# Seven-product blocks for the output projection and the first MLP product, and a norm ahead of its transposes

## The chip, the core and the metric

The kernel runs on one core of a Trainium2 chip. The time is device microseconds of one execution; smaller is better. The core has a matrix engine (TensorE, "PE" in the profile, its weight loads "PEld"), VectorE ("DVE"), ScalarE ("ACT"), GpSimd ("POOL"), and SyncE ("SP"), which issues plain DMAs. GpSimd's queue issues the DMAs that add into their destination. Every engine executes its own instructions in order; semaphores tie the engines together.

## The reference

One layer of a decoder over 512 rows of 1024 columns, all float32:

```python
def rms_norm(x, g):
    y = x * rsqrt(mean(x * x, axis=-1, keepdims=True) + EPS)
    return y * g

def reference(x, ...):
    h = rms_norm(x, norm_mix_g)
    p = h @ w_in                          # 1024 x 8208
    ...                                   # y_a: mLSTM heads, y_b: stick-breaking attention heads, sigmoid gates
    y = gates[..., :D] * y_a + gates[..., D:] * y_b
    x = x + y @ w_out                     # output projection, 1024 x 1024
    h2 = rms_norm(x, norm_mlp_g)
    x = x + square(relu(h2 @ w_up)) @ w_down      # 1024 x 4096, 4096 x 1024
    return x
```

The change touches only the last three lines: the output projection, the second norm, and the two products of the MLP with the way they are interleaved.

## The kernel before

**Numbers.** Every large product is made of three passes: an operand is split into a high part (rounded to the matrix engine's float32r) and a low part (the rest), and `mm3` adds high x high, high x low and low x high. A split costs one copy on ScalarE and one subtraction on VectorE (`stage` for weights, L102 and L103; `parts` in `down`, L695 and L696; `split`, L164 and L165). Weight tiles are 128 x 1024; the pool `wp` has two raw buffers, four of high parts (`whi`) and four of low parts (`wlo`), so weights of two products can stand ready.

**Order.** The framework plans an order for each engine from the program order, a priority and its own estimate of times. A block under `high_priority(offset=AHEAD)` is drawn ahead: weight loads and their splits are. Pools hand out buffers by tag; a new tile of a tag waits until the old tile's last reader is done. `late.close()` ends attention's pool `at`, and the pool `mp` takes over its SBUF.

**Attention's tail.** `ORDER` lists the steps; it ends with heads `s4` to `s7` and the gate chunk `gb1`. A head is a chain: products into `zb`, sigmoids, masks on POOL, scans, a product of vectors, transposes into `zt`, splits into `ah` and `al`, products into `po`, a copy to `yb` (L505). `b_gate_` then multiplies by the gate (L532), adds to `ya` (L533) and splits into `y`. `ya` is the sum of both branches, one 128 x 512 tile for each of eight heads, that is, eight blocks of 128 columns of y, transposed.

**Output projection.** `wo_chunk(half)` makes 512 columns: four row tiles, eight heads each, three passes, 96 matmuls of 128 x 512. The result is added to `acc_t` (L594), four 128 x 1024 tiles that were loaded with x by POOL (L586). A square with an accumulator (L596) gives the row sums of the norm.

**Second norm.** `h2_rows(k)` transposes a block of 128 columns of `acc_t` (L604) and splits it, scaled by the norm's weight (L605, L606). The row factor is applied later: it is spread over a 128 x 512 tile `rw` by products with a diagonal (L632 to L635), and multiplied in when the up product is emptied (L650).

**MLP.** `up(i)` makes 512 of the 4096 hidden columns, transposed, with 96 matmuls of 128 x 512, then relu, square and, for the next step, sums of its quarters. `down(g, u)` multiplies 1024 hidden columns by their 1024 x 1024 of `w_down` and adds to `acc_t`. It uses seven products in place of eight: both matrices are cut into quadrants (A11 to A22, B11 to B22), and each product takes a quadrant or a sum of quadrants. Sums of A are made on VectorE; sums of B by DMAs that add into the raw weight tile (`accum_op`, L719): buffer X holds B11 and then takes in more quadrants, Y holds B22, Z holds B21. `PRODUCTS` lists, for each product, the operand of A, the buffer of B, what is added to it first, and the PSUM tiles (x, z, y), in which products accumulate: 1 and 2 in x, 5 and 3 in z, 6, 7 and 4 in y. Between two products of one PSUM pair the sum so far is read out. `down(g)` yields between products 6 and 7, and there `up(2g + 2)` is put in; `up(2g + 3)` follows.

## Time and profile before

| | |
|---|---|
| runs | 840.05, 840.44, 842.07 us; median 840.44 |
| profiled execution | 838.94 us, span 837.2 us |
| PE busy, matmuls | 823.9 us (98%), 3798 |
| DVE busy | 564.0 us (67%) |
| ACT busy | 408.9 us (49%) |
| POOL busy | 125.9 us (15%) |
| DMA | 98.36 MB, mean 117 GB/s |
| HBM | read 95.52 MB, written 2.17 MB |

The span is the time from the program's first instruction to its last; the execution's time has some 1.7 us around it. Matmuls are pipelined: the duration shown for one includes time in which the next runs already, so the spacing of starts is what a stream costs. A line of the time by stretches gives the stretch, its length, and for each engine the busy time with the number of instructions, then the granted clock of TensorE, the DMA engines' share and their rate. A line in order of time gives start, duration, engine, line of the kernel, operation, out<-in with shapes, and in brackets the idle time ahead of it with what ended it. A line of the groups gives the count, the busy time, the mean duration of one in ns, and the idle time ahead of them. A line of DMA issues gives the tile, the queue, the count, the size of each and the median time from issue to landing.

### The profile page before, as it was taken

The numbers are of one execution on the slowest core, as the hardware profiler recorded it, in microseconds if no ns is written. First come the engines' busy times: TensorE is split into PE (matmuls) and PEld (weight loads), VectorE is DVE, ScalarE is ACT, GpSimd is POOL, SyncE is SP. The second block draws the span as 40 slices with busy tenths as digits, with TensorE's granted clock in tenths as the row PEclk, the third lists the DMA queues.
The fourth block names the chain that finished last, engine by engine and source line by source line (L and its number), as shares of the span: only waits on it lengthen the run. The fifth ranks groups of instructions, "written<-read, shape, count | busy, mean of one in ns | idle before, by whom it ended". The sixth has DMA issues, their size and how long they took to land.

```text
span 837.2 us, 10133 instructions
## 1 busy us (share of the span) xinstructions
PE 823.9 (98%) x3798; PEld 679.3 (81%) x3798; DVE 564.0 (67%) x776; ACT 408.9 (49%) x619; POOL 125.9 (15%) x181
## 2 busy tenths in 40 slices
PE   8999999999999999999999999999999999999997
PEld 5878877788888788888888888888888888888885
DVE  6479997796457786566456446774848475857684
ACT  6338467754436554363345336452545254434441
POOL 3012245142111110010111100020013001300130
PEclk9999999999999999999999999999999999999999
DMA  5163333342113242232122562287438654853374
GB/s 204 53 186 137 111 98 114 105 160 90 55 58 101 60 117 89 88 101 79 50 99 75 184 247 97 80 174 173 141 87 167 160 151 88 170 144 101 51 136 116
DMA packets 56067, 98.36 MB, mean 117 GB/s; under 512 B 4745, under 2 KB 17081, under 8 KB 56018
## 3 DMA queue, kind: packets, MB, share of 16 engines
q1 hardware_dynamic: 45298, 73.51, 27.5%
q0 software_dynamic: 10720, 24.20, 14.7%
q8 instruction: 30, 0.49, 0.2%
q14 instruction: 19, 0.16, 0.1%
HBM read 95.52 MB, written 2.17 MB: 117 GB/s over the span
## 4 chain that ended last, share of the span: by engine, by line
PE 47%; issue 37%; DMA 6%; DVE 5%; POOL 4%; ACT 1%; POOLq 0%; SPq 0%; DVEq 0%; ACTq 0%
DMA raw_X<-in_w_down_dram 5%; PE pp_qkb L107 3%; PE pp_qkb L109 3%; PE pp_qkb L108 3%; POOL raw_X L719 2%; PE pp_ga L107 2%; PE pp_vb L107 2%; PE pp_ga L109 2%; PE pp_ga L108 2%; PE pp_vb L108 2%; PE pp_gb L107 2%; PE pp_oa L107 2%; PE pp_gb L108 2%; PE pp_vb L109 2%; PE pp_oa L108 2%
## 5 line engine op out<-in xcount | busy, mean ns | idle before, releaser
L108 PE MATMUL pp_up<-hT,whi_up 128*128 128x512 f32 x256 | 99.7, 389 | 0.0
L107 PE MATMUL pp_up<-hT,whi_up 128*128 128x512 f32 x256 | 99.4, 390 | 0.0
L109 PE MATMUL pp_up<-hT,wlo_up 128*128 128x512 f32 x256 | 96.2, 389 | 0.0
L719 POOL DMA_DIRECT2D raw_X<-in_w_down_dram x24 | 29.0, 1209 | 287.6 <-DVE wlo_p L696 285.7
L103 DVE TENSOR_TENSOR wlo_up<-raw_up,whi_up 128x1024 fp32r<-128x1024 f32 x32 | 39.2, 1224 | 35.9 <-ACT whi_up L102 35.6
L102 ACT CAST whi_up<-raw_up 128x1024 fp32r<-128x1024 f32 x32 | 33.8, 1055 | 57.6 <-PE y L109 35.6
L109 PEld LDWEIGHTS pp_up<-hT,wlo_up 128*128 128x128 f32 x256 | 48.1, 188 | 10.0
L108 PEld LDWEIGHTS pp_up<-hT,whi_up 128*128 128x128 f32 x256 | 48.1, 188 | 9.9
L107 PEld LDWEIGHTS pp_up<-hT,whi_up 128*128 128x128 f32 x256 | 48.1, 188 | 9.9
L695 ACT CAST whi_p<-raw_X 128x1024 fp32r<-128x1024 f32 x32 | 33.8, 1056 | 37.7 <-PE pp_up L108 24.9
L107 PE MATMUL pp_qkb<-whi_qkb,hT 128*128 128x512 f32 x128 | 50.0, 393 | 0.2 <-DVE va L165 0.2
L482 POOL TENSOR_SCALAR_AFFINE_SELECT b<-b 128x128 f32<-128x128 f32 x32 | 21.2, 679 | 192.7 <-ACT b L479 114.9
L108 PE MATMUL pp_qkb<-wlo_qkb,hT 128*128 128x512 f32 x128 | 50.1, 391 | 0.0
L650 DVE SCALAR_TENSOR_TENSOR ur<-pp_up,rw 128x512 f32<-128x512 f32 x32 | 21.5, 690 | 42.0 <-PE pp_up L109 42.0
L109 PE MATMUL pp_qkb<-whi_qkb,hT 128*128 128x512 f32 x128 | 49.4, 391 | 0.0
L696 DVE TENSOR_TENSOR wlo_p<-raw_X,whi_p 128x1024 fp32r<-128x1024 f32 x32 | 39.1, 1223 | 6.1 <-ACT whi_p L695 5.9
L651 ACT ACTIVATE ur<-ur 128x512 f32<-128x512 f32 x32 | 19.5, 629 | 41.9 <-DVE ur L650 41.6
L487 DVE TENSOR_TENSOR_SCAN r<-r,msk 128x512 f32<-128x512 f32 (+3 forms) x32 | 25.6, 835 | 10.1 <-ACT r L478 10.1
L107 PEld LDWEIGHTS pp_qkb<-whi_qkb,hT 128*128 128x128 f32 x128 | 24.0, 188 | 5.6 <-DVE va L165 0.5
L109 PEld LDWEIGHTS pp_qkb<-whi_qkb,hT 128*128 128x128 f32 x128 | 24.0, 188 | 5.5
L108 PEld LDWEIGHTS pp_qkb<-wlo_qkb,hT 128*128 128x128 f32 x128 | 24.0, 188 | 5.3
L695 ACT CAST whi_p<-raw_Y 128x1024 fp32r<-128x1024 f32 x16 | 16.9, 1053 | 21.5 <-PE x L109 13.8
(290 smaller groups left out, 2310.0 us busy)
## 6 DMA issues: line engine op xcount, KB each, us to landing
raw_up<-in_w_up_dram SPq DMA_DIRECT2D x32, 512.0 KB, 4.0
raw_X<-in_w_down_dram POOLq DMA_DIRECT2D x24, 512.0 KB, 6.3
raw_qkb<-in_w_in_dram SPq DMA_DIRECT2D x32, 256.0 KB, 3.8
rb<-rows POOLq DMA_DIRECT2D x8, 640.0 KB, 4.9
raw_va<-in_w_in_dram SPq DMA_DIRECT2D x8, 512.0 KB, 6.5
raw_qka<-in_w_in_dram SPq DMA_DIRECT2D x16, 256.0 KB, 4.3
raw_vb<-in_w_in_dram SPq DMA_DIRECT2D x8, 512.0 KB, 4.0
raw_oa<-in_w_in_dram SPq DMA_DIRECT2D x8, 512.0 KB, 3.9
```

The source lines that it names most:

```text
L102: act.copy(hi, raw)
L103: dve.tensor_sub(lo, raw, hi.bitcast(F32))
L107: pe.matmul(o, ah, bh, start=start, stop=False, **kw)
L108: pe.matmul(o, ah, bl, start=False, stop=False, **kw)
L109: pe.matmul(o, al, bh, start=False, stop=stop, **kw)
L482: pool.affine_select(out=b[:, d], in_=b[:, d], pattern=[[-1, P]], compare_op=ALU.is_gt, fill=0.0, base=0, channel_multiplier=1)
L487: dve.tensor_tensor_scan(kr, kr, msk[:, S - n:][:, ::-1], 1.0, ALU.mult, ALU.max)
L650: dve.scalar_tensor_tensor(u[:, w, :], acc[j + 2 * w], 0.0, rw, ALU.max, ALU.mult)
L651: act.activation(u[:, w, :], u[:, w, :], AF.Square)
L695: act.copy(hi, t)
L696: dve.tensor_sub(lo, t, hi.bitcast(F32))
L719: pool.dma_start(out=buf[b, j], in_=src(more, j), accum_op=ALU.add)
```

## The change

- A function `wino` does one block of seven products for any weights, in the order 1, 2, 5, 3, 6, 7, 4. The output projection is one such block (168 matmuls of 128 x 512), each of the four groups of 1024 hidden columns one for the up product and one for the down product. In the up block the weights are the stationary operand and 256 rows stream: 48 matmuls of 128 x 256 for a product.
- `ya` becomes two tiles `yq` of 128 x 4 x 512 (heads 0 to 3, and 4 to 7). A11 and A12 are the first 256 rows of each. `rows_ops` makes A22, S1, S4, S2 and S3 in place, with four sums and five splits of 128 x 1024.
- The row factor of the second norm is applied to `acc_t` (a new tile `xh`) ahead of the transposes, for 256 rows at a time: rows 0 and 1 after product 6 of the projection, rows 2 and 3 after product 4. `rw` and its products go.
- The transposed rows go to `hq`, the up product is emptied into `uq`; `yq`, `hq` and every `uq` share the tags `ya0` and `ya1`, with one buffer each.
- `up` and `down` follow one another without interleaving in the program order. The raw buffers in `mp` go from eight to six; the block's first-freed weights (X in the projection, Z elsewhere) use the two raw buffers of `wp`.
- GpSimd's space for DMA descriptors is set to 4096.

```diff
+TARGET = {2: ((0, 0), 1), 5: ((1, 1), 1), 3: ((0, 1), 1), 6: ((0, 1), -1), 7: ((1, 1), -1), 4: ((1, 0), 1)}
+ORDER_W = (1, 2, 5, 3, 6, 7, 4)
+DONE = {2: (0, 0), 6: (0, 1), 7: (1, 1), 4: (1, 0)}
...
+    yq = [big.tile([P, 4, S], F32, tag=f"ya{c}", name=f"yq{c}") for c in range(2)]
+    ya = [yq[h // 4][:, h % 4, :] for h in range(8)]
...
+        a = f"A1{i + 1}"
+        Y[a] = rows_split(r4_pair(f"y{a}"), y_quad(0, i))      # at the end of b_gate_
...
+    def rows_split(pair, val):
+        hi, lo = pair
+        act.copy(hi, val)
+        dve.tensor_sub(lo, val, hi.bitcast(F32))
+        return pair
...
+    def wino(name, src, A, rows, emit, small, psum, first_load=None):
+        buf, sums = {}, {}
+        with ExitStack() as es:
+            es.enter_context(tc.high_priority(offset=AHEAD))
+            if first_load is not None:
+                es.enter_context(tc.issue_after(first_load))
+            for b, n in (("X", "B11"), ("Z", "B21"), ("Y", "B22")):
+                for j in range(2):
+                    pool_, tag, bufs = (wp, "raw", 2) if b == small else (mp, "rawd", 6)
+                    buf[b, j] = pool_.tile([P, 2, S], F32, tag=tag, name=f"raw_{b}{name}{j}", bufs=bufs)
+                    last["load"] = nc.sync.dma_start(out=buf[b, j], in_=src(n, j)).ins
...
+        for n in ORDER_W:
+            a, b, more, to = PRODUCTS[n]
+            with tc.high_priority(offset=AHEAD):
+                if n > 3:
+                    for j in range(2):
+                        pool.dma_start(out=buf[b, j], in_=src(more, j), accum_op=ALU.add)
+                w = [parts(f"p{n}{name}{j}", buf[b, j]) for j in range(2)]
+            start = to not in sums
+            if start:
+                sums[to] = [psum(f"{to}{name}{t}") for t in range(2)]
+            hi_a, lo_a = A[a]
+            for t in range(2):
+                for p in range(4):
+                    (hi, lo), kk = w[p // 2], p % 2
+                    if rows:
+                        sl = slice(t * P, (t + 1) * P)
+                        mm3(sums[to][t], hi_a[:, p, sl], lo_a[:, p, sl], hi[:, kk, :], lo[:, kk, :], ...)
+                    else:
+                        for o in range(2):
+                            sl = slice((2 * t + o) * P, (2 * t + o + 1) * P)
+                            mm3(sums[to][t][:, o * HT:(o + 1) * HT], hi[:, kk, sl], lo[:, kk, sl], hi_a[:, p, :],
+                                lo_a[:, p, :], ...)
+            for t in range(2):
+                emit(n, t, sums[to][t])
+            yield n
+
+    def rows_ops(A, q, tile):
+        A["A22"] = rows_split(tile("A22"), q(1, 1))
+        dve.tensor_sub(q(1, 1), q(1, 0), q(1, 1))
+        A["S1"] = rows_split(tile("S1"), q(1, 1))
+        dve.tensor_sub(q(1, 0), q(0, 0), q(1, 0))
+        dve.tensor_sub(q(0, 0), q(1, 1), q(0, 0))
+        dve.tensor_add(q(0, 1), q(0, 1), q(0, 0))
+        A["S4"] = rows_split(tile("S4"), q(0, 1))
+        A["S2"] = rows_split(tile("S2"), q(0, 0))
+        A["S3"] = rows_split(tile("S3"), q(1, 0))
...
+    def wo_emit(n, t, p):
+        for q, sign in SIGN_1.items() if n == 1 else [TARGET[n]]:
+            add(quad(*q, t), p, sign)
...
+    def h2_rows(r):
+        xh = []
+        for t in (2 * r, 2 * r + 1):
+            n = mp.tile([P, D], F32, tag="xh", name=f"xh{t}", bufs=2)
+            ss = sm.tile([P, 1], F32, tag="r1", name=f"ss{t}")
+            act.activation(n, acc_t[t], AF.Square, accum_out=ss)
+            act.activation(ss, ss, AF.Sqrt, scale=1.0 / D, bias=eps)
+            dve.reciprocal(ss, ss)
+            dve.tensor_scalar_mul(n, acc_t[t], ss)
+            xh.append(n)
+        ...                    # 16 transposes into four banks, eight scaled copies of 128 x 256 into hq
+
+    rows_ops(Y, y_quad, lambda name: r4_pair(f"y{name}"))
+    for n in wino("wo", weights(w_out, 0, 0), Y, True, wo_emit, "X", pp):
+        if n == 6:
+            h2_rows(0)
+            for c in range(2):
+                a = f"A1{c + 1}"
+                H2[a] = rows_split(h2_tile(a), h_quad(0, c))
+    wo_load = last["load"]
+    h2_rows(1)
+    rows_ops(H2, h_quad, h2_tile)
...
+    def up(g):
+        uq = [big.tile([P, 4, S], F32, tag=f"ya{c}", name=f"uq{g}{c}") for c in range(2)]
+        ...
+        def emit(n, t, p):
+            ...
+            if n == 1:
+                act.copy(h(1, 0), p)
+            elif n == 2:
+                act.activation(h(0, 0), p, AF.Relu)
+            elif n == 5:
+                dve.tensor_sub(h(1, 1), p, h(1, 0))
+            ...                # 3, 6, 7, 4: one sum or difference on VectorE each
+            if t == 1 and n in DONE:
+                ...            # maximum with 0 on VectorE, square on ScalarE, split of A11 and A12
+        for _ in wino(f"up{g}", weights(w_up, 0, g * D), H2, False, emit, "Z", pp, wo_load if g == 0 else None):
+            pass
+        rows_ops(U, q, tile)
+        return U
...
     for g in range(4):
-        nu = []
-        for _ in down(g, u):
-            nu += up(2 * g + 2)
-        u = nu + up(2 * g + 3) if g < 3 else []
+        down(g, up(g))
...
-    nc = _bacc.Bacc("TRN2", target_bir_lowering=False, num_devices=1)
+    nc = _bacc.Bacc("TRN2", target_bir_lowering=False, num_devices=1, dynamic_dma_scratch_size=4096)
```

211 lines of the change are left out of this document (89 added, 122 removed), and 3 rows, old and new, of the table PRODUCTS.

## The prediction

> **What bounds the kernel now.** I read the page's engine table and slices first, then the time by stretches, then the order of instructions in time at the two places that the change rebuilds.
>
> ```profile
> PE 823.9 (98%) x3798; PEld 679.3 (81%) x3798; DVE 564.0 (67%) x776; ACT 408.9 (49%) x619; POOL 125.9 (15%) x181
> PE   8999999999999999999999999999999999999997
> PEclk9999999999999999999999999999999999999999
> ```
>
> TensorE is busy 823.9 of 837.2 us, in every slice but the first and last, at full clock. So each matmul taken away is worth its spacing, provided that nothing else then runs dry. A matmul's duration (389 ns for 512 columns) overlaps its neighbour's; what counts is the spacing of starts.
>
> ```profile
> core 0: us, PE busy (x) PEld busy (x) DVE busy (x) ACT busy (x) POOL busy (x), PEclk, DMA share, GB/s
> 580.00:620.00 40.00, 40.00 (x178) 33.14 (x177) 22.26 (x34) 15.64 (x23) 0.00 (x0) 1.00 0.41 127
> 792.50:833.60 41.10, 39.27 (x170) 31.23 (x168) 30.19 (x42) 14.90 (x18) 7.27 (x6) 1.00 0.65 134
> ...
> 239.44 0.28 PE L107 MATMUL po<-ah,vb 128*128 128x256 f32 x1
> 239.56 0.29 PE L108 MATMUL po<-al,vb 128*128 128x256 f32 x1
> 239.68 0.28 PE L109 MATMUL po<-ah,vb 128*128 128x256 f32 x1
> 239.80 0.39 PE L384 MATMUL za<-qh,kk 128*128 128x512 f32 x1
> ...
> 465.19 0.28 PE L107 MATMUL po<-ah,vb 128*128 128x256 f32 x1
> 465.30 0.28 PE L108 MATMUL po<-al,vb 128*128 128x256 f32 x1
> 465.42 0.28 PE L109 MATMUL po<-ah,vb 128*128 128x256 f32 x1
> 465.53 0.22 PE L107 MATMUL po<-ah,vb 128*128 128x128 f32 x1
> ```
>
> The first window holds only 512-column matmuls: 40.00/178 = 0.225 us each. Three 256-column ones take 0.36 us at 239.44 and 0.34 us at 465.19: 0.113 to 0.12, mean 0.117, a little over half. The second window is the last down block, the only seven-product block with no up chunk beside it.
>
> **The change part by part.** *TensorE work.* The output projection goes from 2 chunks x 4 x 8 x 3 = 192 matmuls to 7 products x 2 x 4 x 3 = 168, all of 512 columns: 24 x 0.225 = 5.4 us less. The up product goes from 8 x 96 = 768 of 512 columns (172.6 us) to 4 groups x 7 products x 48 = 1344 of 256 columns: 1344 x 0.117 = 157 us, 15.6 less (ends: at 0.12, 11.3 less; at 0.113, 20.7). So seven products of eight bring 9%, not 12.5%, since a half-width matmul costs more than half. The transposes stay 32; the products that made rw go:
>
> ```profile
> L634 PE MATMUL prw<-dg,ones 128*128 128x128 f32 x8 | 1.1, 274 | 0.0
> ```
>
> Together 5.4 + 15.6 + 1.1 = 22.1 us less. In a kernel that is 98% TensorE that would be 818. The rest asks what TensorE then waits for.
>
> [...]
>
> *Ahead of the output projection.* Now the tail of attention is covered by it: head 7 is a chain of transposes, copies and sums, and the projection's products over heads 0 to 6 fill TensorE meanwhile.
>
> ```profile
> 451.90:457.30 5.40, 5.36 (x23) 4.13 (x23) 0.00 (x0) 1.00 0.03 9
> 451.90:475.00 23.10, 20.68 (x89) 16.41 (x90) 0.52 (x1) 1.00 0.27 97
> ...
> 466.63 0.69 DVE L532 TENSOR_TENSOR g_gb<-g_gb,yb 128x512 f32<-128x512 f32 x1 [4.78 <-ACT yb L505]
> 467.36 0.69 DVE L533 TENSOR_TENSOR ya<-ya,g_gb 128x512 f32<-128x512 f32 x1
> ...
> 468.69 2.13 POOL L586 DMA_DIRECT2D acc<-in_x_dram  x4 [16.62 <-issue]
> ...
> 477.13 0.69 DVE L594 TENSOR_TENSOR acc<-acc,pp_wo 128x512 f32<-128x512 f32 x1 [1.37 <-DMA acc<-in_x_dram]
> 478.45 0.69 DVE L594 TENSOR_TENSOR acc<-acc,pp_wo 128x512 f32<-128x512 f32 x1 [0.63 <-DMA acc<-in_x_dram]
> ```
>
> The first two rows count the projection's matmuls alone: 20.68 us of them between 451.9 and 475. Afterwards only product 1 (A11, heads 0 to 3) is possible before head 7's y is added at 468.05, because A12 and all sums need heads 4 to 7: 24 x 0.225 = 5.4 us. The remaining 15.3 us of cover are gone. Work resumes near 475: from 468.05, two copies on ScalarE of A12 and A22 and, on VectorE, A12's and A22's low parts, one difference, then S1's copy and low part:
>
> ```profile
> L696 DVE TENSOR_TENSOR wlo_p<-raw_X,whi_p 128x1024 fp32r<-128x1024 f32 x32 | 39.1, 1223 | 6.1 <-ACT whi_p L695 5.9
> L695 ACT CAST whi_p<-raw_X 128x1024 fp32r<-128x1024 f32 x32 | 33.8, 1056 | 37.7 <-PE pp_up L108 24.9 <-PE z L109 4.8 <-PE x L109 4.8
> 636.11 1.23 DVE L696 TENSOR_TENSOR wlo_p<-raw_X,whi_p 128x1024 fp32r<-128x1024 f32 x1
> 637.25 0.69 DVE L165 TENSOR_TENSOR ta<-sa,ta 128x512 fp32r<-128x512 f32 x1
> 637.85 0.69 DVE L165 TENSOR_TENSOR tb<-sb,tb 128x512 fp32r<-128x512 f32 x1
> ```
>
> 1.06, three VectorE steps at their spacing of 1.14 (636.11 to 637.25), 1.06 and 1.22: 468.05 + 6.8 = 474.8, when product 5 can start. Its added weights need an adding load on POOL's queue, which holds little there: head 7's masks before 452 and the four acc loads, 2.13 us. Product 2 is no earlier. Its weights (Z) lie in pool mp, whose first load was issued at 468.69, right after attention's last read of the SBUF that mp takes over; and it adds into product 1's banks, which must first be emptied into acc, whose last rows landed about 477 and 478, with Z and Y, which wait on SP's queue for the same release, now loading beside them. So I take 15.3 us lost; ends 10 (head 7 sooner, ScalarE and VectorE having fewer copies of y beside it) and 22 (product 2 first, at 482).
>
> *The second norm.* Now each block of columns is transposed unscaled and the row factor is applied after the up product, so no matmul waits for the norm. Then it stands ahead of the transposes. Rows 0 and 1 are done under products 7 and 4 (10.8 us). Rows 2 and 3 start when product 4 ends:
>
> ```profile
> L594 DVE TENSOR_TENSOR acc<-acc,pp_wo 128x512 f32<-128x512 f32 x8 | 5.4, 686 | 9.5 <-PE pp_wo L109 7.5 <-DMA acc<-in_x_dram 2.0
> L216 ACT ACTIVATE jk<-x 128x1024 f32<-128x1024 f32 x4 | 4.2, 1060 | 2.7 <-DMA x<-in_x_dram 2.7
> L217 ACT ACTIVATE r<-r,eps 128x1 f32<-128x1 f32 x4 | 1.2, 295 | 0.2
> L218 DVE RECIPROCAL r<-r 128x1 f32<-128x1 f32 x4 | 0.6, 157 | 4.6 <-ACT r L217 4.6
> L334 DVE TENSOR_SCALAR cy<-xc,vec 128x512 f32<-128x512 f32 x8 | 4.1, 528 | 2.8 <-ACT xc L328 2.8
> L604 PE MATMUL p<-ident,acc 128*128 128x128 f32 x32 | 4.6, 272 | 0.0
> L654 ACT CAST ue<-ur 128x256 fp32r<-128x256 f32 x32 | 11.2, 397 | 0.0
> ```
>
> Matmul's end 0.4, add 0.7, square 1.06, its accumulator 0.2, root 0.3, reciprocal 0.16, scaling of 1024 columns about 1.0, first transposes 0.7, eight copies at 0.4: quadrants complete 7.6 us after product 4. Then nine VectorE operations of 1.14 (four differences and sums, five low parts; the price of 128x1024 above), one copy ahead and two weight splits between: 12.5 + 1.06, so the last sum is split at about +21. The up block can run products 1 and 5 meanwhile (2 x 48 x 0.117 = 11.2) and 16 transposes (about 1.6), but not product 2: product 1's banks are emptied into uq, which has the SBUF tag of hq with a single buffer, so that copy waits until the last operand is split from hq. Cover 12.8, wait 21.6 with the copy: 9 us lost. Ends: 0 (uq free as soon as S1 is there, at about +13) and 14.6 (product 5 not drawn ahead of product 2, another 5.6).
>
> *Seven-product up blocks.* The 256-column products come every 5.6 us and each needs two weight splits (2 x 1.06 on ScalarE, 2 x 1.14 on VectorE). An up and a down block together: 28 weight splits, seven operand splits and four sums, all at 1.14 = 44.5 us, plus 23 emptyings at the 0.6 from 637.25 to 637.85 and three maxima of 1024 at about 1.0 (twice the 0.53 of L334) = 16.8: 61.3 us of VectorE in 77 us, 80%. In the last down block, at 30.19/41.10 = 73%, TensorE lost 41.10 - 39.27 = 1.8 us. I take that for the four up blocks, 7 us; the down blocks have an up block's first product behind them as filler, as now. Ends: 0 and 12.6 (the other three down blocks too).
>
> *DMAs.* Up and projection weights gain 8 adding loads per block in place of plain ones:
>
> ```profile
> raw_X<-in_w_down_dram POOLq DMA_DIRECT2D x24, 512.0 KB, 6.3
> q1 hardware_dynamic: 45298, 73.51, 27.5%
> q0 software_dynamic: 10720, 24.20, 14.7%
> ```
>
> An adding load lands 6.3 us after issue; from the split of a product's weights to the same buffer's next is two products, 11 us, less the split's 2.4: hidden, with 2 us to spare. Shares: 40 more on q0 (21 MB, +13%), 10 fewer on q1 (5 MB, -2%): 42 to 53% over the span, no bound by itself. POOL issues 8 x 1.2 us per block; nothing else stands in that queue then. At nothing, covered by those 11 us; without, it is in the blocks' upper end. The smaller descriptor space for POOL's DMAs shows in no row; 0, at worst the 2 us of slack per block, inside the same end.
>
> **Sum.** Against the profiled execution's 838.9: -22.1 + 15.3 + 9 + 7 = +9.2, so 848; the median of the runs shown is 1.5 above that execution, so 849.6.
>
> **The rivals.** *Head 7 ends early, or the planner closes the gap ahead of the projection* (not slower): TensorE's empty slots let heads 5 to 7 move up some 13 us, and 2 us are lost there. Against it: the last head's steps wait on ScalarE, POOL and VectorE in turn, not on TensorE (VectorE's 4.78 us wait is for yb). 849.6 - 13.3 = 836; it decides once the three losses fall under 22 us together.
>
> *The norm's gap closes:* the planner draws S1 ahead and uq is free in time: 840.6. For it: operands of rows 0 and 1 are ready early; against it: one buffer per tag.
>
> *The 256-column spacing falls in long streams to the shortest single step shown, 0.11* (465.19 to 465.30): 147.8 us of up products, 9.2 less, so 840.4. Against it: both triples, as wholes, are longer. [...]
>
> *VectorE becomes the bound of the MLP:* at 80% in order, each of the four pairs of blocks loses 6 us, 24 in place of 7: 866.6. For it: the last down block loses time already at 73%.
>
> A further cost: a waiting TensorE could lose its clock. The first matmuls of the kernel show what a slow one takes:
>
> ```profile
> L202 PE MATMUL pw<-warm 128*128 128x512 f32 x5 | 2.5, 661 | 1.5 <-DVE warm L173 1.5
> ```
>
> The granted clock never falls later, as no idle stretch is long. [...]
>
> **How the numbers follow.** Forecast (gaps of about these sizes) 0.55, its own range 843 to 857; gap at the projection closed 0.12; norm's gap closed 0.1; short spacing 0.08; VectorE bound 0.15. Within 0.3% is 837.9 to 843, about what a measurement of this kernel can tell from no change. Faster: the first rival and some of the two that end near 840, 0.18. Same: the rest of those, 0.15. Slower: the forecast and the last, 0.67. Range 835 to 867: from the first rival to the last, without what lies beyond either.
>
> **What would show it.** 1344 matmuls of 256 columns at 0.117 us; TensorE busy about 802; a window of some 15 us between the end of gb1's matmuls and 475 with one product in it; after the last matmul of the projection, product 5 before product 2 and ScalarE's copy into uq waiting for the split of hq; VectorE near 75% from there on; waits of matmuls for weight splits. Wrong if TensorE stays at 98%, or if the blocks lose more than the two gaps.

## The result: 4.3% slower

The changed kernel takes 876.84 us (median; 875.47 to 877.13), the kernel before, beside it, 840.25 (839.77 to 842.07): ratio 1.0428, interval 1.0409 to 1.0447. The forecast was 849.6, in a range of 835 to 867. The sign was right; the time lies 9.8 us above the range.

The page of the changed kernel (engine table and slices), profiled at 876.93 us:

```profile
span 875.2 us, 11352 instructions
PE 819.4 (94%) x4342; PEld 699.6 (80%) x4342; DVE 624.6 (71%) x759; ACT 451.3 (52%) x605; POOL 173.5 (20%) x220
PE   8998998999999999999994795999999999899978
PEclk9999999999999999999997798999999999999999
```

TensorE's busy time hardly fell (823.9 to 819.4), its share fell from 98 to 94%, and the granted clock dips where the slices fall to 4, 7 and 5. A dip inflates busy time: a 128x512 matmul of product 5 lasts 0.63 us at a granted clock of 0.50 (490.31) and 0.39 at 1.00 (493.82), and does no more. The view of TensorE's waits (for whom, at which line; total, times, longest) names the places:

```profile
PE pp_zwo L108 <- ACT yS1h L548: 11.4, 1, 11.4
PE pp_zup L108 <- ACT h L548: 7.3, 1, 7.3
...
PE zdn L108 <- ACT uS41h L548: 2.1, 1, 2.1
PE zdn L108 <- ACT uS40h L548: 2.1, 1, 2.1
PE zdn L108 <- ACT uS42h L548: 2.1, 1, 2.1
PE zdn L108 <- ACT uS43h L548: 2.1, 1, 2.1
PE zdn L110 <- DVE uS13l L549: 2.1, 1, 2.1
PE pp_zwo L110 <- DVE yS1l L549: 2.0, 1, 2.0
```

Every row is a matmul that waits for a sum of A: the first six for its copy on ScalarE (S1 in the first two, S4 in the next four), the last two for S1's low part on VectorE. The first two rows are the two gaps of the forecast. The four rows with S4 are one wait in each down block, where the forecast had none. (The rows left out between are attention's; the largest, 4.8 us ahead of head 7's transposes, lies in the first gap too.)

**The books.** The spans differ by 875.2 - 837.2 = 38.0 us. Up to the end of the projection (its last matmul starts at 500.21 before, at 525.72 after, and the first up product follows at 500.7 and 527.4) 26.7 are lost: attention ends 7.9 later, 24 matmuls fewer save 5.4, and 24.2 are lost cover. From there to the end (336.5 before, 347.8 after) 11.3 are lost: about 15.4 less work in the up blocks and 26.7 more of other time, nearly all waits and slow clock.

### The projection

The changed kernel in order of time, ScalarE, VectorE, TensorE (start, duration, engine, line, operation, tiles; in brackets the idle time before and its releaser):

```profile
479.52 1.05 ACT L634 CAST whi_p2wo<-raw_Zwo 128x1024 fp32r<-128x1024 f32 x1 [1.56 <-DMA raw_Zwo<-in_w_out_dram]
481.30 1.05 ACT L634 CAST whi_p2wo<-raw_Zwo 128x1024 fp32r<-128x1024 f32 x1 [0.73 <-DMA raw_Zwo<-in_w_out_dram]
482.25 1.99 ACT L634 CAST whi_p5wo<-raw_Xwo 128x1024 fp32r<-128x1024 f32 x2
484.15 1.04 ACT L548 CAST yS1h<-yq 128x1024 fp32r<-128x1024 f32 x1
...
475.24 0.69 DVE L535 TENSOR_TENSOR yq<-yq,g_gb 128x512 f32<-128x512 f32 x1
479.44 1.23 DVE L668 TENSOR_TENSOR yq<-yq,yq 128x1024 f32<-128x1024 f32 x1
488.01 1.23 DVE L549 TENSOR_TENSOR yS1l<-yq,yS1h 128x1024 fp32r<-128x1024 f32 x1
...
489.29 0.80 PE L110 MATMUL pp_zwo<-whi_p5wo,yS1l 128*128 128x512 f32 x1 [1.98 <-DVE yS1l L549]
490.31 0.63 PE L109 MATMUL pp_zwo<-wlo_p5wo,yS1h 128*128 128x512 f32 x1
490.74 0.63 PE L110 MATMUL pp_zwo<-whi_p5wo,yS1l 128*128 128x512 f32 x1
```

Head 7's y is complete at 475.93, 7.9 us later than the 468.05 of before. S1's sum is complete at 480.67. Its copy, in ScalarE's order behind four copies of weights, two of which wait for Z's DMA, starts only at 484.15. The low part follows at 488.01, in VectorE's order behind the splits of product 5's weights. Product 5 starts at 485.24, waits once more, and its matmuls come every 0.43 us (490.31 to 490.74), where the granted clock is 0.50 (476.3 to 493.4), in place of 0.23 from 493.82 on, where it is 1.00.

### The second norm and a down block

The norm (ScalarE, then VectorE, then ScalarE):

```profile
542.45 1.05 ACT L548 CAST h<-hq 128x1024 fp32r<-128x1024 f32 x1 [2.55 <-DVE hq L668]
...
549.34 1.23 DVE L549 TENSOR_TENSOR h2S4l<-hq,h2S4h 128x1024 fp32r<-128x1024 f32 x1
...
549.38 1.08 ACT L750 COPY uq<-pp_xup 128x512 f32<-128x512 f32 x2
```

The first row is the copy of S1, for which product 5 waits. The copy from product 1's banks into `uq` starts at 549.38, beside the last split from `hq` (S4's), not before: the single buffer of the tag, as forecast.

A down block, the one of the second group (VectorE, then ScalarE), two stretches of it, and one of the last down block:

```profile
676.93 1.23 DVE L672 TENSOR_TENSOR uq<-uq,uq 128x1024 f32<-128x1024 f32 x1
...
678.66 1.23 DVE L635 TENSOR_TENSOR wlo_p6dn<-raw_Xdn,whi_p6dn 128x1024 fp32r<-128x1024 f32 x1
...
678.59 1.05 ACT L634 CAST whi_p6dn<-raw_Xdn 128x1024 fp32r<-128x1024 f32 x1 [0.26 <-PE zdn L110]
679.54 1.04 ACT L548 CAST uS41h<-uq 128x1024 fp32r<-128x1024 f32 x1
...
676.00:681.00 5.00, 2.92 (x14) 2.10 (x13) 5.00 (x6) 3.47 (x4) 2.78 (x3) 1.00 0.70 114
681.00:684.60 3.60, 3.60 (x10) 2.79 (x9) 3.60 (x4) 1.48 (x2) 1.64 (x2) 0.53 1.12 200
849.30:851.30 2.00, 2.00 (x9) 1.47 (x10) 2.00 (x3) 1.85 (x2) 1.31 (x2) 1.00 1.16 179
```

VectorE is busy without a break (5.00 of 5.00, 3.60 of 3.60). The sum S4, which product 3 needs next, is complete at 678.16; its copy stands on ScalarE behind the copy of product 6's weights, which themselves have to wait for TensorE to be done with product 5 (678.59). Product 3 starts 2.1 us late, at 680.64, and the clock from 681.0 to 684.6 is 0.53. The waits for S4 in the first and third group are followed by half clock too (0.50 from 599.2 to 602.6 and from 763.0 to 766.4). The last one, as long (2.08 us, until 849.29), is not: the clock behind it is 1.00.

Why the sums come so late shows beside the kernel before. In order of time, in VectorE's rows of one group: the first of these sums after an emptying, the last emptyings of the up product, and the last low part of a sum (kernel before, then the changed one):

```profile
622.05 0.42 DVE L663 TENSOR_TENSOR sb<-ur 128x256 f32<-128x256 f32 x1
629.18 1.28 DVE L650 SCALAR_TENSOR_TENSOR ur<-pp_up,rw 128x512 f32<-128x512 f32 x2
637.85 0.69 DVE L165 TENSOR_TENSOR tb<-sb,tb 128x512 fp32r<-128x512 f32 x1
```

```profile
663.13 0.68 DVE L762 TENSOR_TENSOR uq<-uq,pp_yup 128x512 f32<-128x512 f32 x1
667.79 1.22 DVE L668 TENSOR_TENSOR uq<-uq,uq 128x1024 f32<-128x1024 f32 x1
683.80 1.23 DVE L549 TENSOR_TENSOR uS31l<-uq,uS31h 128x1024 fp32r<-128x1024 f32 x1
```

Before, the sums are made quarter by quarter, the first ones while the up product still runs, and the last split starts 8.7 us after the last emptyings. After, the quadrant (1,0), which S1, S2, S3 and S4 all need, is complete only with product 4, the last of the up block; all sums are made behind it, and the last split starts 20.7 us after the last emptying.

### The profile page after: what moved, and what is told of

Its sections match the earlier page's. It is cut to its first block, busy times and chain, and to the rows that moved or that the text cites. A ratio compares the mean times of both kernels' runs of the same rounds, so it can differ in the third digit from the quotient of the medians.

```text
span 875.2 us, 11352 instructions
## 1 busy us (share of the span) xinstructions
PE 819.4 (94%) x4342; PEld 699.6 (80%) x4342; DVE 624.6 (71%) x759; ACT 451.3 (52%) x605; POOL 173.5 (20%) x220
## 4 chain that ended last, share of the span: by engine, by line
PE 71%; issue 10%; DVE 10%; ACT 4%; DMA 2%; POOL 2%; POOLq 0%; DVEq 0%; ACTq 0%
PE ydn L108 3%; PE ydn L109 3%; PE pp_qkb L108 3%; PE pp_qkb L109 3%; PE pp_qkb L110 3%; PE ydn L110 2%; PE zdn L108 2%; PE pp_yup L110 2%; PE pp_yup L108 2%; PE pp_yup L109 2%; PE zdn L110 2%; PE pp_zup L109 2%; PE zdn L109 2%; PE pp_xup L109 2%; PE pp_zup L110 2%
## 5 line engine op out<-in xcount | busy, mean ns | idle before, releaser
L643 POOL DMA_DIRECT2D raw_Xup<-in_w_up_dram x24 | 28.7, 1196 | 118.4 <-DVE wlo_p1up L635 68.2
L110 PE MATMUL pp_qkb<-whi_qkb,hT 128*128 128x512 f32 x128 | 49.4, 391 | 0.0
L643 POOL DMA_DIRECT2D raw_Xdn<-in_w_down_dram x24 | 28.7, 1196 | 103.9 <-DVE wlo_p1dn L635 47.7
L108 PE MATMUL pp_qka<-hT,whi_qka 128*128 128x512 f32 x64 | 25.7, 404 | 3.2 <-ACT xc L329 3.2
L108 PE MATMUL pp_va<-whi_va,hT 128*128 128x512 f32 x64 | 25.8, 404 | 0.0
L109 PE MATMUL pp_qka<-hT,whi_qka 128*128 128x512 f32 x64 | 25.8, 403 | 0.0
L108 PE MATMUL pp_zup<-h,whi_p5up 128*128 128x256 f32 x64 | 18.7, 298 | 7.3 <-ACT h L548 7.3
L109 PE MATMUL pp_va<-wlo_va,hT 128*128 128x512 f32 x64 | 25.6, 400 | 0.0
L110 PE MATMUL pp_va<-whi_va,hT 128*128 128x512 f32 x64 | 25.4, 402 | 0.0
L108 PE MATMUL pp_ga<-hT,whi_ga 128*128 128x512 f32 x64 | 25.1, 395 | 0.0
L108 PE MATMUL pp_oa<-hT,whi_oa 128*128 128x512 f32 x64 | 25.1, 392 | 0.0
L109 PE MATMUL pp_gb<-hT,whi_gb 128*128 128x512 f32 x64 | 25.0, 391 | 0.0
L109 PE MATMUL pp_vb<-wlo_vb,hT 128*128 128x512 f32 x64 | 25.0, 391 | 0.0
L109 PE MATMUL pp_ga<-hT,whi_ga 128*128 128x512 f32 x64 | 25.0, 390 | 0.0
L108 PE MATMUL pp_gb<-hT,whi_gb 128*128 128x512 f32 x64 | 24.9, 390 | 0.0
```

The lines of the kernel that those rows point to most:

```text
L108: pe.matmul(o, ah, bh, start=start, stop=False, **kw)
L109: pe.matmul(o, ah, bl, start=False, stop=False, **kw)
L110: pe.matmul(o, al, bh, start=False, stop=stop, **kw)
L643: pool.dma_start(out=buf[b, j], in_=src(more, j), accum_op=ALU.add)
```

## The experiments

Ratios are to the kernel before on the same chip. "Changed kernel" is the one of the diff above.

### Why does attention end later?

The first suspect was the only edit that reaches so far forward, the space for DMA descriptors: alone in the kernel before, and enlarged in the changed kernel.

```diff
-    nc = _bacc.Bacc("TRN2", target_bir_lowering=False, num_devices=1)
+    nc = _bacc.Bacc(..., dynamic_dma_scratch_size=4096)     # in the kernel before
-    ... dynamic_dma_scratch_size=4096)
+    ... dynamic_dma_scratch_size=8192)                      # in the changed kernel
```

> The kernel before, with one line of the change alone: GpSimd's space for DMA descriptors set to 4096. Theory (the smaller space is what makes attention, whose instructions are in the same order in both kernels, 6.3 us late by 92 us): about 846.5 us, rows of rb landing near 6.5 us after issue in place of 4.9, first masks near 65.7 us in place of 61.9. Rival (the lateness comes from the changed tiles or from another DMA load): within 1 us of the kernel before, 840.3, and rb's rows at 4.9 us.

> The changed kernel with GpSimd's space for DMA descriptors at 8192 in place of 4096, nothing else. Theory (descriptor space delays the rows of rb early in attention): 3 to 6 us less than 876.8, rb landing near 4.9 us, POOL's idle time put down to DMA rb back to some 20 us. Rival (space plays no part there): 876.8 within 1 us.

Measured: 840.06 against 840.06 (ratio 0.9992, 0.9975 to 1.0008); and 876.28, 1.0436 (1.0417 to 1.0456). The descriptor space costs nothing and is not the cause. The next suspects were the size of a table in DRAM and the order in which the input arrays are laid out:

```diff
-    rows = dram.tile([8, LIN], F32, name="rows")
+    rows = dram.tile([72, LIN], F32, name="rows")[:8, :]    # in the changed kernel
...
+    for name in sorted(_INS, key=lambda n: n == "w_in"):    # w_in declared last, in the version "c_tuned" below
```

> The changed kernel with the DRAM tile rows of 72 rows in place of 8, of which 8 are used. Theory (the packets of w_in take longer because of where the changed program places it in memory): a shift of 328 KB may change the DMA share of the first 100 us from 0.50 towards 0.42 and take up to 7.9 us off. Rival (another cause, or a shift that does not matter): 876.8 within 1 us and a share of 0.50.

> As c_tuned, with w_in declared as the last of the inputs in place of the third. Theory (the place of w_in in memory sets how long its packets take, and the place follows this order): DMA share of the first 100 us near 0.42 and 6 to 8 us less than c_tuned; or another share, if the new place is no better. Rival (the place does not follow this order, or does not matter): c_tuned's time within 1.5 us and a share of 0.50.

Measured: 878.41, 1.0448 (1.0427 to 1.0469), and 861.36, 1.0251 (1.0222 to 1.0281) against 1.0228 without that edit; the DMA engines' share in the first 100 us stayed at 0.49 in both. Neither edit brings the time back; whether they moved `w_in` in the chip's memory, no run shows. What was left was the length of the program, since the versions with the old projection are slow there too: the kernel before with 600 small matmuls (64 columns) appended, and the changed kernel without its last group, which leaves a quarter of the MLP out.

```diff
+    more = bank("more")                                     # in the kernel before, at its end
+    with tc.issue_after(last["mm"]):
+        for i in range(600):
+            pe.matmul(more[:64, :64], one, one, start=True, stop=True)
...
-    for g in range(4):                                      # in the changed kernel
+    for g in range(3):
         down(g, up(g))
```

> The kernel before with 600 matmuls of 64 columns more after its last one, whose results are thrown away, so that the program is about as long for TensorE as the changed one (4392 matmuls in place of 3792; 4340 in the changed kernel). Only the first 470 us are read, the tail costs some 35 to 40 us more. Theory (a longer program moves w_in to a place in memory where its packets take longer): DMA share of the first 100 us 0.50 in place of 0.42, head 7's y added near 476 in place of 468. Rival (something else in the changed kernel): 0.42 and 468.

> The changed kernel without the last of the four groups of hidden columns (its output lacks that part), 3836 matmuls. Only the first 470 us are read; the whole is some 82 us shorter. Theory (length of the program): DMA share of the first 100 us 0.42, head 7's y added near 468. Rival: 0.50 and 476.

One execution each: 876.5 with its tail, and 790.4. The page's row of SyncE's queue for the first 100 us (packets, MB, share of 16 engines), of the kernel before, the changed one, the long one before, the short one after:

```profile
q1 hardware_dynamic: 9778, 11.61, 35.8%
```

```profile
q1 hardware_dynamic: 9506, 11.08, 44.2%
```

```profile
q1 hardware_dynamic: 9506, 11.08, 44.0%
```

```profile
q1 hardware_dynamic: 9778, 11.61, 35.3%
```

The long version of the kernel before has the changed kernel's slow transfers, the short version of the changed kernel the fast ones, with less moved in the same time in the slow ones. Head 7's last add starts at 467.36, 475.24, 473.83 and 469.92 in that order. By their pages the four have 3798, 4342, 4398 and 3838 matmuls: the slow transfers follow the length of the program, not what is changed in it, and with them most of the delay (6.5 us in the long version; 2.6 remain in the short one). The change pays for it because it has 544 matmuls more. How length comes to slow packets of the first 100 us stays open (the theory of the expectations, that it moves `w_in` in memory, is shown by no run); descriptor space, the size of the table in DRAM and the order of the inputs make no difference.

### How much is the projection's?

The changed kernel with the eight-product projection of before (up blocks and norm as changed):

```diff
-    rows_ops(Y, y_quad, lambda name: r4_pair(f"y{name}"))
-    for n in wino("wo", weights(w_out, 0, 0), Y, True, wo_emit, "X", pp):
+    list(wo_chunk(0))
+    for n, _ in enumerate(wo_chunk(1)):
```

> The changed kernel with the projection of the kernel before (eight products, two halves of the columns, heads split one by one); norm and MLP as changed. Theory (the seven-product projection gives up the cover of attention's tail: 5.4 us of matmuls saved, some 15 of waiting and 5 of halved clock lost): TensorE has work from 454 to the end of the projection, which ends near 509 in place of 526; 15 to 18 us less, 859 to 862. Rival (head 7's chain sets the time in any case): under 6 us less, 871 or more.

Measured: 858.66, 1.0227 (1.0207 to 1.0247), 18.2 us less than the changed kernel; the first up product starts at 509.92 in place of 527.45, 17.5 sooner. So nearly the whole difference lies ahead of that start, and half of the loss is the new projection's. Its attention is late as well (head 7's last add at 474.81), which fits the length: it has 4366 matmuls.

How much of it is clock: 70 matmuls without use, from product 1's operands into product 5's banks, fill the gap of the changed kernel.

```diff
+            if name == "wo" and n == 1:
+                sums["z"] = [psum(f"z{name}{t}") for t in range(2)]
+                ...                                          # 18 at once, 52 behind head 7's last product
+                    pe.matmul(sums["z"][0], hi_a[:, i % 4, :P], hi_a[:, 0:2, :], start=True, stop=True)
```

> The changed kernel with 70 matmuls of 128x512 more, whose results are thrown away, in the gap ahead of the projection: 18 before head 7's transposes, 52 after its last product (15.8 us at 0.225, in some 17 of waiting). Theory (the granted clock halves after the waits, so product 5 runs at twice its time when it starts): the 24 matmuls of product 5 take about 7.5 us (5.4 and the wait of 2.0 for S1's low part) in place of 10.7, 3 us less, 874. Rival (product 5 is slow because its operands arrive late): 876.8 or, if the added matmuls stand in the way, some more.

Measured: 874.18, 1.0417 (1.0392 to 1.0442). The time by stretches, of the changed kernel and of this one:

```profile
454.30:485.20 30.90, 14.74 (x72) 12.67 (x70) 19.20 (x24) 13.44 (x21) 4.74 (x8) 0.75 0.27 99
485.20:501.00 15.80, 13.78 (x47) 10.64 (x48) 15.63 (x18) 5.88 (x6) 4.14 (x4) 0.74 0.95 275
```

```profile
454.30:485.20 30.90, 29.92 (x146) 24.41 (x144) 20.08 (x26) 13.55 (x21) 4.75 (x8) 1.00 0.30 112
485.20:501.00 15.80, 13.13 (x57) 10.53 (x58) 15.80 (x18) 6.96 (x7) 4.86 (x4) 1.00 0.92 255
```

At full clock the second stretch holds 57 matmuls in place of 47, but the time gained is 2.7 us, less than the intervals of the two ratios resolve; in the traces the first up product starts 2.1 us sooner (525.31 for 527.45). The clock is a small part of the gap, and the operands, which come hardly sooner (product 5 starts at 484.55 for 485.24), are the rest.

### What the blocks wait for

In the changed kernel the down products read A11 and A12 in place of every other operand, so that nothing waits for sums (the output is another one; all work is still done):

```diff
-        down(g, up(g))
+        U = up(g)
+        down(g, {n: U["A12" if n in ("A12", "S4", "S3") else "A11"] for n in U})
```

> The changed kernel, with the down products reading A11 or A12 of their block wherever they read S1, S4, S2, S3 or A22; the sums and splits are still all made, so VectorE, ScalarE and the DMAs do the same work, but no down product waits for a sum (the output is not the reference's). Theory (each of the four down blocks loses about 5 us because the last sums of A are split late, behind splits of later weights, and TensorE is then at half clock for 3.4 us): 18 to 20 us less, near 857, four down blocks of about 37.8 us each. Rival (the down blocks are bound by VectorE's work as a whole, or by weights that arrive late through DMA engines busy at 0.86): the waits move to the weights' low parts, gain under 5 us, 872 or more.

Measured: 866.24, 1.0314 (1.0299 to 1.0329): 10.6 us less, not as much as expected. The first matmul of two successive up blocks, in the changed kernel and here, and the same point of two successive pairs in the kernel before:

```profile
701.42 0.28 PE L108 MATMUL pp_xup<-h,whi_p1up 128*128 128x256 f32 x1
783.80 0.28 PE L108 MATMUL pp_xup<-h,whi_p1up 128*128 128x256 f32 x1
```

```profile
696.08 0.28 PE L108 MATMUL pp_xup<-h,whi_p1up 128*128 128x256 f32 x1
774.85 0.28 PE L108 MATMUL pp_xup<-h,whi_p1up 128*128 128x256 f32 x1
```

```profile
574.09 0.39 PE L107 MATMUL pp_up<-hT,whi_up 128*128 128x512 f32 x1
656.17 0.39 PE L107 MATMUL pp_up<-hT,whi_up 128*128 128x512 f32 x1
```

A pair of up and down block lasts 82.4 us in the changed kernel and 78.8 here; before it lasted 82.1, so the changed kernel loses in each pair all that its up block saves. The pair's matmuls alone take about 336 x 0.117 + 168 x 0.2265 = 77.4. So about 5 us are lost per pair, 3.6 of them to operands that are sums.

Could a better order bring those sums sooner? First by priority, then written out: product 5's matmuls ahead of product 2's in the projection; in the down blocks product 6's weights behind S4's split, and the second half of the emptying of product 5 too.

```diff
+        with tc.high_priority(offset=AHEAD):                # first version: all of rows_ops
+            rows_ops_(A, q, tile)
...
-        for n in ORDER_W:                                   # second version
+        for n in (1, 5, 2, 3, 6, 7, 4) if name == "wo" else ORDER_W:
...
+            key = LATER.get((name[:2], n[1]))               # LATER = {("dn", "6"): "S4"}
+                if key:
+                    es.enter_context(tc.issue_after(last[key + "h"]))
                 act.copy(hi, t)
```

> The changed kernel with the sums of A and their splits (of y, of the normed rows, of the hidden columns) drawn ahead with the same priority as the weight splits. Theory (the sums stand behind splits of later weights in VectorE's and ScalarE's order): the projection's gap shrinks by some 3.5 us, the second norm's by some 3, each down block by some 2.5: 15 us less, near 862. Rival (the planner's own order of these steps is as good as another, what counts is the sum of VectorE's work between the last emptying and the third product): within 3 us of 876.8.

> The changed kernel with three pieces of order set by hand and no work added or removed: in the projection, product 5 stands before product 2 in the program, so its weights are split first and S1's copy is not behind the weights of product 2; in each down block, the weights of product 6 are split only after S4, and the second half of product 5 is emptied after S4's split. Theory (each down block's loss of some 5 us, and some 4 us of the projection's gap, come from work that stands ahead of S4 and S1 in ScalarE's and VectorE's order, with the halved clock behind each wait): 3 to 5 us less per down block and 4 to 5 less ahead of the projection, 16 to 25 in all, 852 to 861. Rival (VectorE is full there, an order only moves the wait to another operand): the down period stays at 82 us, gain under 6 us, 871 or more.

Measured: 877.06, 1.044 (1.0423 to 1.0457): the order of VectorE and ScalarE stayed the same, so priority says nothing here. And 871.89, 1.0379 (1.0351 to 1.0407): 5.0 us less, where 16 to 25 were expected (the rival's bound, 871 or more, holds). A pair lasts 80.2 in place of 82.4, its waits for S4 are of 0.5 to 1.1 us, and behind them the matmuls of the first three groups last 0.39 to 0.40 us (in the second the granted clock is 1.00 from 655 to 700). Nearly half of a pair's loss is thus one of order. In the projection S1's copy still started at 484.50, behind product 2's copies, and though product 5's 24 matmuls took 8.6 us in place of 10.7, the first up product starts at 528.30, no sooner than the 527.45 of the changed kernel: the new order gained nothing there.

The norm's gap: quadrant (1,0) of the up product in a tile of its own, so that product 1's banks can be emptied while `hq` is still being read.

```diff
+        u10 = mp.tile([P, 4, HT], F32, tag="u10", name=f"u10{g}")
         def q(r, c):
+            if (r, c) == (1, 0):
+                return u10[:, :, :]
```

> The changed kernel with a tile of its own for the quadrant (1,0) of the up products, in place of a part of the tile that shares its buffer with the normed rows. Theory (product 1's emptying waits for the last split of the normed rows because of the single buffer, so product 2 cannot fill the wait for S1): product 2 runs before product 5 and covers 5.6 of the 7.7 us of waiting at 535.9 to 543.6, and the clock stays up: 6 to 8 us less, 869 to 871. Rival (product 2 waits for something else as well, the weights of Z or ScalarE's order): within 2 us of 876.8.

Measured: 874.25, 1.0401 (1.0374 to 1.0428), 2.6 us less, under half of what was expected. The intervals of the two ratios overlap, but the trace shows the gain: from the first up product to the first of the next down block it is 46.2 us (528.05 to 574.26) in place of 49.4 (527.45 to 576.81). Product 2 did run in the gap (its matmuls up to 542), and product 5 then still waited 1.97 us (to 545.04) for S1's copy and 2.41 for its low part: the buffer was one limit, the norm's chain the next.

VectorE's load taken down: in the down blocks, on top of the written order, GpSimd makes the low parts of the weights of products 5 and 3.

```diff
-                dve.tensor_sub(lo, t, hi.bitcast(F32))
+                on = pool if name[:2] == "dn" and n[1] in "53" else dve
+                on.tensor_sub(lo, t, hi.bitcast(F32))
```

> As a_order_ops, and the low parts of the weights of products 5 and 3 of each down block (four subtractions of 128x1024 a block) are made by GpSimd in place of VectorE. Theory (VectorE has no idle time while S1 to S4 are made, so what counts is how much else stands in that stretch): 4.6 us of VectorE's work leave the stretch, the remaining waits of some 3 us a down block go, 8 to 12 us less than a_order_ops, 860 to 864. Rival (the waits are for the split's copy on ScalarE or for the added weights): within 3 us of a_order_ops, 871.9; if GpSimd's subtractions are late or hold up its adding loads, slower.

Measured: 897.87, 1.0673 (1.0652 to 1.0694), 26 us more than without it. GpSimd, then VectorE, of one down block:

```profile
676.34 2.90 POOL L644 TENSOR_TENSOR wlo_p5dn<-raw_Xdn,whi_p5dn 128x1024 fp32r<-128x1024 f32 x1
...
680.38 5.10 POOL L644 TENSOR_TENSOR wlo_p3dn<-raw_Ydn,whi_p3dn 128x1024 fp32r<-128x1024 f32 x2
...
676.32 4.01 DVE L680 TENSOR_TENSOR uq<-uq 128x1024 f32<-128x1024 f32 x1
...
680.85 5.72 DVE L550 TENSOR_TENSOR uS11l<-uq,uS11h 128x1024 fp32r<-128x1024 f32 x1
```

GpSimd's subtractions take 2.4 to 2.9 us, and a subtraction of VectorE that runs beside them takes 4.01 and 5.72 us in place of 1.22: in both cases it ends 1.1 us after GpSimd's, as if it had waited for them and then taken its own time. What it waited for the trace does not name; VectorE's sum with the PSUM tile `xdn` at 673.01, beside GpSimd's subtraction of 672.79 to 675.19, took 0.69 us, as such sums do in this block (0.67 to 0.69). Work moved from VectorE to GpSimd came back on VectorE.

### Versions put together

The first one takes the old projection, the own tile for quadrant (1,0) and the written order in the down blocks; the second adds GpSimd's low parts and a DRAM table of 1000 rows.

> The changed kernel with the projection of the kernel before, a tile of its own for quadrant (1,0), and the order of the down blocks of a_order_ops. Theory (the losses stand in different places and add up): 858.7 of a_old_projection less 2.6 of a_own_q10 less some 5 for the order: 850 to 852. Rival (the waits are one queue of VectorE's work, so that what is gained in one place is lost in the next): 855 or more.

> As c_old_projection_q10_order, with the low parts of products 5 and 3 of the down blocks on GpSimd, and with the DRAM tile rows of 1000 rows (5.1 MB) in place of 8, of which 8 are used. Theory for the first: 8 to 12 us less, 840. For the second: if the place of w_in in the chip's memory sets how long its packets take, another layout may give attention's 7.9 us back (832) or not; if w_in's packets are slow for another reason, the first 100 us stay as in the changed kernel (DMA share 0.50, in the kernel before 0.42). Rival for the whole: 848 or more.

Measured: 852.31, 1.0144 (1.0122 to 1.0166): the three gains nearly add up (18.2 + 2.6 + 5.0 = 25.8 one by one, 24.5 together). And 878.09, 1.0442 (1.0425 to 1.046), with the DMA share still at 0.50: GpSimd's part takes back 25.8, as it took 26 without the table. A third version starts from the first and gives product 5's first weights of a down block buffers of their own:

```diff
+            if name[:2] == "dn" and n[1] == "5" and n[-1] == "0":
+                hi, lo = [mp.tile([P, 2, S], F32R, tag="xh", name=f"w{w}_{n}", bufs=2) for w in ("hi", "lo")]
...                              # norm's weights of product 2 behind the norm; s1 added late in the last block
```

> As c_old_projection_q10_order (852.3), with three changes of order: product 5's first weights of each down block are split into the two buffers that xh leaves free, so that the splits of products 5 and 3 can be made earlier; the weights of product 2 of the first up block are split after the last row's norm; in the last down block the sums of product 1 over the four groups are added to the output's quadrants after product 3. Theory (what is left is an order: VectorE has room earlier in the block): 3 to 5 us at the norm, 1 to 2 per down block, 4 to 6 in the last, 838 to 844. Rival (VectorE's work between the end of the up block and S4 is the bound): 849 or more.

Measured: 858.37, 1.0228 (1.019 to 1.0266), 6 us more than the first. With the added buffers the weights of products 5 and 3 are split earlier in the planner's order, ahead of work that TensorE needs sooner; from the first down block to the second it takes 84.6 us (555.55 to 640.17) in place of 81.3, and products 1 and 2 of the second block 16.7 (640.17 to 656.83) in place of 14.7 (637.90 to 652.58). A miss.

The fourth gives TensorE something to do while S1 and S4 are made: product 1 of the next up block is put between products 2 and 5 of the down block, with the first version's edits and the last two small ones of the third.

```diff
-        down(g, up(g))
+        V = {}
+        nxt = up(g + 1, V) if g < 3 else iter(())
+        for n in down(g, U):
+            if n == FILLER:                                  # FILLER = 2
+                next(nxt, None)
+        list(nxt)
+        U = V
```

> As c_old_projection_q10_order, with product 1 of each next up block put between products 2 and 5 of the down block in the program, and with the last two changes of c_tuned (norm ahead of product 2's weights, sums of product 1 after product 3 in the last block), without its extra buffers. Theory (S1 and S4 only lack cover: 5.6 us of matmuls against 2.3 us more of weight splits): the waits of 2.7 us in each of three down blocks go, the norm gains 1.4 and the last block 2.5: 852.3 less 12, 840 to 843. Rival (VectorE's work as a whole, some 80% in order, is the bound): the down period stays near 80.5 us, 848 or more.

Measured: 843.96 (842.01 to 844.57), 1.0045 (1.0027 to 1.0063), 8.4 us less than the first version, where some 12 were expected. Its page:

```profile
PE 817.2 (97%) x4366; PEld 699.6 (83%) x4366; DVE 603.6 (72%) x740; ACT 440.9 (52%) x600; POOL 164.7 (20%) x212
```

VectorE's and ScalarE's load is that of the first version; TensorE is at 97%, and in the first three down blocks only one wait is left, of 0.83. So VectorE's time as a whole was not the bound of the down blocks; late sums without cover were. A pair now lasts 77.95 us (the first matmul of product 5 of the second up block starts at 609.55, that of the third at 687.50) against 82.1 before: here the seven-product up block does pay, some 4 us a pair. What keeps this version behind the kernel before is the later attention (head 7's last add starts at 472.24 against 467.36) and the waits at the norm and in the last down block. The last version orders the norm's operands anew on top of it: S1 in a tile of its own and split first, A22 last, half of the scaled copies on VectorE, product 3's weights behind S1 and product 6's behind S4.

```diff
+        s = mp.tile([P, 4, HT], F32, tag="xh", name=f"s1{name}", bufs=2)[:, :, :]
+        dve.tensor_sub(s, q(1, 0), q(1, 1))
+        A["S1"] = rows_split(tile("S1"), s)
...
+        A["A22"] = rows_split(tile("A22"), q(1, 1), last["S4h"], last["S4"])
```

> As c_interleaved, with S1 in a tile of its own (one of xh's two buffers), the split of A22 moved behind those of S1, S4, S2 and S3, half of the scaled copies into hq on VectorE, the weights of the first up product 1 split into four buffers of r4 (not behind the projection's weights), weights of products 3 and 6 of that block split after S1 and S4, and the late sums of the last block issued after S4. No matmul is added or taken away. Theory (what is left at the norm and in the last down block is things that stand in front of S1 and S4): A11 2 us and S1 3 to 5 us earlier, less time at half clock, 1 to 2 us in the last block: 843.9 less 4 to 7, 837 to 840, level with the kernel before (840.1) or under it. Rival (the chain add, square, root, scaling, transposes, copies, sums is what counts): 842 or more.

Measured: 851.33, 1.0152 (1.0138 to 1.0166), a miss by 11 us and more. S1 did come sooner (product 5 starts at 520.46 in place of 525.78). But:

```profile
531.15 1.22 DVE L652 TENSOR_TENSOR wlo_p6up<-raw_Xup,whi_p6up 128x1024 fp32r<-128x1024 f32 x1
532.28 1.28 DVE L791 TENSOR_TENSOR uq<-pp_zup,u 128x512 f32<-128x512 f32 x2
...
533.11 0.55 PE L110 MATMUL pp_zup<-h2S4h,whi_p3up 128*128 128x256 f32 x1 [6.73 <-DVE uq L791]
```

The emptying of product 5 now stands in VectorE's order behind five more operand and weight splits, and product 3, which needs its banks, waits 6.73 us; in the last down block a matmul of product 7 waits 5.1 for an emptying. The wait was moved, not removed. No version beats the kernel before.

## Why the prediction was right in its sign and wrong in its size

**Right: the work.** 24 matmuls less in the projection and 1344 narrow ones, at the spacing forecast (5.44 us for the 48 of some products, 5.76 for others, 0.113 to 0.12 us each, mean 0.117). "In a kernel that is 98% TensorE that would be 818. The rest asks what TensorE then waits for" was the right question. VectorE's load came as worked out: 61.80 us in a pair where 61.3 were forecast, 75% of the pair's 82.38. No matmul waits for an adding load, and the descriptor space costs 0, as taken. Two of the signs named did not come: the waits are not for weight splits but for sums of A, and TensorE's busy time is not 802 but 819.4, as the slow clock (0.971 in the mean, against 1.0 before) swells it. Three of the rivals did not come: no head moved up, neither gap closed, the mean spacing did not fall to 0.11. The fourth, VectorE as bound of the MLP, came near in size (24 us foreseen, some 21.5 lost) but not in cause: with VectorE's load unchanged, early operands bring a pair's loss down to 1.4, and the interleaved version runs at 97%.

**Wrong by 7.9: attention was taken as untouched.** The sum has no term for it, and resumed "from 468.05". It ends at 475.93, for the most part because the longer program has slower transfers at its start (a share of 44.2% in the first 100 us against 35.8, for less data): 6.5 of the 7.9 come with length alone, and 2.6 remain without it, in one execution of each. Nothing in the trace of before shows it.

**Wrong by 8.9: the projection's lost cover,** 24.2 in place of 15.3, above its upper end of 22. With head 7 later by 7.9 its "Work resumes near 475" would be 482.7; it was 485.24. The step counted S1's chain as if ScalarE and VectorE had nothing else: its copy stood behind copies of Z's weights, which the same paragraph had named as late, and its low part behind product 5's splits. Then product 5 ran at half clock (0.50 granted from its start to 493.4) with a second wait, 10.66 us in place of 5.4. The sum has no term for the clock; the fill experiment gives 2 to 3 us for this gap alone. In the down blocks, four of the five waits of 2.1 us were followed by half clock, 3.41 us of it each time, so the cost is paid in every group. The forecast's "as no idle stretch is long" does not settle when the clock falls: before, it was 1.00 up to 836 us, beside the first matmuls of 0.66 us and through a wait of 2.25 us (until 11.04) too, while here 2.08 us were followed by half clock in the first three groups and 2.07 (until 840.80) in the fourth, but 2.08 until 849.29 were not; what decides is not shown.

**Wrong by 12.0: the MLP,** in three terms, sized from starts of matmuls less their number times their spacing. The norm cost 11.4 in place of 9, within its ends; the mechanism (`uq` behind the last split from `hq`) is in the trace, yet only some 3 of it came back with a tile of its own. The up blocks cost 0 in place of 7. The down blocks cost some 21.5 (4.1, 5.0 and 5.0 in the first three, 7.4 in the last) in place of 0. That makes 17 more than forecast; some 5 of it, by difference, the kernel before loses in this part too, and the sum had counted it as free of loss. The failed step is "the down blocks have an up block's first product behind them as filler, as now". It fails twice. The filler behind is not where the waits are: of the next up block the planner draws only the first matmuls forward, into product 4 (701.42 and 703.21 in the second group), while TensorE waits ahead of product 3. And "as now" does not hold: before, an up chunk stood between products 6 and 7 by program order, also behind products 5 and 3; these did not wait because their sums were ready early. The change makes the sums late (20.7 us after the last emptying in place of 8.7), and the step has no term for that, though `rows_ops` stands behind the whole up block in the diff. Two experiments show it: with operands that are no sums 10.6 us go, and with a product put in front of product 5 8.4 go. A wait of 2.08 and 3.4 us at half clock (1.7 lost) make 3.8 of a pair's 5; that split is worked out, not measured.

**Open.** Why the program's length reaches the first transfers; what decides whether a wait of 2 us costs the clock; and how far the norm's gap can be brought down, since the own tile took 2.6 and the new order only moved it.

## What to carry to other kernels

Cheaper products are worth their spacing only while something else can run: before taking work away, list for every operand that is a sum when its last part is complete and what TensorE does until it is split, and put a product of the next block there, by program order. A chain's price is not its instructions' sum but that sum behind everything its engines have queued ahead; an engine at 71% can still be late with the one thing that counts. And a wait can cost its clock as well: here four of five waits of 2.1 us were followed by 3.41 us at 0.50, which makes an estimated 3.8 us of each 2.1, nearly twice what the wait view shows.

## What the hardware showed

- A longer program (4342 or 4398 matmuls against 3798 or 3838) raised the share of the plain DMA queue in the first 100 us from 35.8 and 35.3% to 44.2 and 44.0% for less data (11.08 MB against 11.61), and the last head's last add came 5.3 us (changed kernel against its short version) and 6.5 us (kernel before with and without the tail) later, in one execution of each edited version.
- In the changed kernel the granted clock fell to 0.50 after four of five waits of 2.1 us in the down blocks and stayed there for 3.41 us; behind waits of 0.5 to 1.1 us, in the version with the written order, the matmuls of three groups kept their 0.39 to 0.40 us.
- Beside GpSimd's subtractions of 2.4 to 2.9 us, two of VectorE's took 4.01 and 5.72 us in place of 1.22, in the version with GpSimd's low parts.
